# Starting the prompt's attention inside the even layer's last projection unit

## The chip, the core and the metric

The kernel runs on one core of a Trainium2 chip. The metric is device time in microseconds (us) for one execution. TensorE is PE in the profile (PEld is its weight load), VectorE is DVE, ScalarE is ACT, GpSimd is POOL; SP is the engine whose queue issues nearly all DMAs.

## The reference, cut to what matters

One inference step of two layers, on a prompt of 2048 tokens and on 8 sequences of 4 new tokens ("the sample"). The even layer projects its input to a linear-attention branch (A) and to q, k, v, a gate and a forget value of four heads of "forgetting attention" (B, called fox in the code). The odd layer is another linear attention. The part that matters here is the prompt's forgetting attention:

```python
proj = h @ w_in                                  # even layer, all branches
log_fb = log_sigmoid(fb + b_fox)
c = cumsum(log_f, axis=1)                        # per head, over the 2048 tokens
logits = einsum('bthd,bshd->bhts', qi, k) * scale + ci[..., None] - c[:, :, None, :]
logits = where(t >= key_pos, logits, -inf)
p = softmax(logits)
out = einsum('bhts,bshd->bthd', p, v)
```

The sample's attention does the same for its 32 tokens against 128 cached pages of k and of v, read from memory by a page table.

## The kernel before, in words

**Stages.** `phase_even` (L949) computes the even layer's projections in two halves of the tokens, `phase_fox` (L1118) both attentions, `phase_odd` (L1768) the even layer's output projection and the odd layer. A float32 product is made of three float16 products (`mm3`, L468 to L472: high by high, high by low, low by high), so most matmuls of the profile stand at L470, L471 and L472.

**The even layer's units.** Each half runs 16 units of weight columns, in the list `order` of `phase_even`; the last four of it are Bk0, Bv0, Bk1 and Bv1: the keys and values of heads 0 and 1, then those of heads 2 and 3. `staged` (L1044) yields after each piece of a unit and fetches, measures and splits the weights of later units between the pieces. `dense(a, b)` is units a to b - 1 of the half. Of the second half's Bv1, the last unit of all, there are four pieces of 48 matmuls of 128x256 (`proj_tm`); each piece is copied out of PSUM by DVE (L893), and DVE takes its largest value (L902, `vmax`); SP stores it to the output and to `vd` (L907, L910).

**Sums of log f.** When the forget values are there (from Bv0), `log_sigmoid` (L1098) runs; after unit Bk1, `bias_rows` (L1083) makes the cumulative sums with two small matmuls (`cum` L1089, `cumo`), scales them on DVE and stores 64 rows to `cbd` (L1096). The attention reads them back, broadcast, into `cb` (L1165).

**The prompt's attention.** `fox_prompt` (L1153) goes over 16 groups: four heads by four groups G of 512 queries. For group (h, G) it loads q, k, v (`raw`), the bias `cb` and the gate (L1139, L1165, L1174), splits each into two float16 tiles (ACT L1148 and L1149, POOL L1150), and runs four blocks of 128 queries. A block of `scores` (L1185) is G + 1 tiles `s` of up to 512 keys on PE; DVE adds the bias, writes `L` and keeps the maximum (L1203, one pass a tile, two for the tile on the diagonal, where POOL made `cm` from bias and mask, L1189); ACT takes the exponential (L1211); POOL divides by the sum (L1219). `values` (L1222) of the group before runs between these blocks: PE transposes `L` into `pt` (L1239), ACT and DVE split that into `th` and `tl` (L1246, L1247), PE multiplies by v into `fo`. There are two PSUM buffers for `s` and two for `pt`. Group (0, 0) has only four short tiles, group (0, 1) two tiles a block, and so on.

**The sample's attention.** `fox_sample` (L1306) loads pages of k (L1333), transposes each set of four pages on PE (`pkt`, L1363), copies it to SBUF on ACT and DVE (`kts`, L1366 and L1367) and multiplies (`sc`, L1421); later it does the weighted sum over pages of v (`pv`, L1502), with few operations beside PE. Before its first product, DVE scales its q and k (`qs`, `kn`, L1351) and spreads q (`qz`, L1355). Its page buffers (`fs`) lie where the even layer's activations and weights lay.

**What sets the order.** `until(a, ta, b, tb)` (L92) and `mux` draw steps from two generators so that their yielded costs stay in the ratio ta to tb; `until` stops when b ends. This gives each instruction a place in the program; the framework's scheduler then orders every engine's queue by that place and by when it expects inputs to be there. Each engine runs its queue in order. Before, `drain(until(self.prompt, FOX_P, self.fox_sample(fs, pps), FOX_S))` pairs prompt and sample; what is left of the prompt then goes beside `prepare` (in `phase_odd`), which readies the first weights and inputs of the output projection.

**Memory.** Tile pools are stacks on a left and a right side of SBUF, and PSUM has eight banks. Before, all pools of the even layer close together after Bv1, and the attention's pools open then. The attention's `s` tiles take PSUM banks that the projections' `pj` tiles had, so the first `s` waits for the last copies of Bv1.

Of the kernel before, what the change touches and what calls it, by code (L numbers as in the profile page):

```python
# [8 lines left out]
F32 = mybir.dt.float32  # L9
# [6 lines left out]
ALU = mybir.AluOpType  # L16
PSUM = bass.MemoryType.PSUM
DRAM = bass.MemoryType.DRAM

P = 128  # L20
# [19 lines left out]
EWR = 3  # L40
# [8 lines left out]
PG = 25  # L49
# [3 lines left out]
NG = 2  # L53
WSPLIT = 4
FOX_S = 411000.0
FOX_P = 270000.0
LIN3_A = 40000.0
LIN_E = (20000.0, 15000.0)
LIN_O = (31000.0, 23000.0)
# [5 lines left out]
FAR = -3e38  # L65
# [9 lines left out]
def mux(a, ta, b, tb):  # L75

    pa = pb = 0.0
    la = lb = True
    while la or lb:
        if la and (not lb or pa * tb <= pb * ta):  # L80
            c = next(a, None)
            la = c is not None
            pa += c or 0
        else:
            c = next(b, None)
            lb = c is not None
            pb += c or 0
        if c:
            yield c


def until(a, ta, b, tb):  # L92

    pa = pb = 0.0
    while True:
        first = pa * tb <= pb * ta
        c = next(a if first else b, None)
        if c is None and not first:
            return
        if first:  # L100
            pa += c or 0
            if c is None:
                yield from b
                return
        else:
            pb += c
        yield c


def drain(g):  # L110
    for _ in g:
        pass
# [9 lines left out]
class Kern:  # L122
# [825 lines left out]

    def phase_even(self):  # L949
        tc, nc, i = self.tc, self.nc, self.i  # L950
        def pool(name, **kw):
            return tc.tile_pool(name=name, bufs=1, reuse_waits="tile", **kw)

        with pool("act", side="right") as ap, pool("w", side="right") as w0, pool("wl", side="right") as wp1, \
                pool("wk") as wp0, pool("nrm") as n0, pool("stt") as sp, pool("ps", space=PSUM) as pp0:
            wpool = Pool(w0, {"w": 3, "wr": EWR, "rm": 2, "pow": 2, "lr": 8})
            wp = Pool(wp0, {"c4": 7, "sam": 1, "v4": 3, "sg": 3, "pd": 1, "kt": 2, "y": EY, "xpad": 1, "vs": 3,
                            "ss": 2, "rs_t": 2, "rs_r": 2}, Pool(wp1, {"c2": EC2, "th": ETH}))
            pps = Pool(pp0, {"pj": 3, "gr": 2, "st": 1, "o": 2})
            nrm = Pool(n0, {"th": 1, "nss": 4, "rs_t": 4, "rs_r": 4})  # L960
            self.scales2, self.ready, self.fsc, self.logit, self.v_undo = {}, {}, {}, {}, {}
            self.sx_even = self.gain_scale(self.g_even, pps, "pj", "e")
            S1 = sp.tile([P, P], F32, name="Sx")
            S = [(sp.tile([P, P], F32, name=f"S{h}"), S1) for h in range(NH)]
            act = self.alloc_act(ap)
            self.few = wp
            last = iter(())
            order = ["v0", "g0", "qf0", "qf1", "Bq0", "Bg0", "v1", "g1", "qf2", "qf3", "Bq1", "Bg1",
                     "Bk0", "Bv0", "Bk1", "Bv1"]
            us, lins = [], []  # L970

            def beside(x):
                x -= 33
                for n in (1, 2):
                    if 0 <= x - 1 < len(self.later):
                        self.later[x - 1][n]()
                if 0 <= x < len(self.later):
                    self.later[x][0]()

            self.later = []  # L980
            for hf in range(2):
                U, lin = self.even_half(hf, act, wpool, wp, pps, nrm, S)
                us += [U[x] for x in order]
                lins.append(lin)
            for hf in range(2):
                def get_x(c0, m, hf=hf):
                    t = wp.tile([P, HALF + TS], F32, tag="c4", name=f"nx{hf}_{c0}")[:, :D]
                    src = i["x_prompt"][0, hf * HALF + c0 : hf * HALF + c0 + m] if c0 < HALF else \
                        i["x_sample"].rearrange("b t d -> (b t) d")
                    self.last_x = nc.sync.dma_start(t[:m], src)  # L990
                    return t

                def dense(a, b, hf=hf):
                    return self.staged(us, 16 * hf + a, 16 * hf + b, beside)

                lin = lins[hf]
                groups = self.norm_groups(nrm, pps, act, hf, get_x, self.g_even)
                first = self.handover(groups, dense(0, 1), last)
                if hf == 0:
                    groups[0][0]()  # L1000
# [24 lines left out]
                drain(dense(14, 15))  # L1025
                if hf == 1:
                    self.bias_rows(pps, *masks)
                last = dense(15, 16)
            drain(last)

    def later_units(self):
        i = self.i
# [85 lines left out]
    def phase_fox(self):  # L1118
        tc, nc = self.tc, self.nc
        self.fox = ExitStack()  # L1120
        f1, f0 = (self.fox.enter_context(tc.tile_pool(name=x, bufs=2, reuse_waits="tile")) for x in ("fe", "fx"))
        pp1, pp0 = (self.fox.enter_context(tc.tile_pool(name=x, bufs=2, space=PSUM, reuse_waits="tile"))
                    for x in ("fpa", "fpb"))
        if True:
            fx = Pool(f0, {"vh": 5, "vl": 5, "P": 17, "th": 4, "tl": 4, "sg": 3, "y": 1},
                      Pool(f1, {"raw": 6, "caus": 1, "qh": 2, "ql": 2, "kh": 5, "kl": 5, "cb": 2, "st1": 12, "cm": 2}))
            pps = Pool(pp0, {"t": 2, "o": 1, "kt": 2}, Pool(pp1, {"s": 2, "sc": 1}))
            caus = fx.tile([P, P], F32, tag="caus", name="caus")
            nc.gpsimd.memset(caus, 0.0)
            nc.gpsimd.affine_select(caus, caus, [[-1, P]], ALU.is_ge, FAR, base=0, channel_multiplier=1)  # L1130
            with tc.tile_pool(name="fs", bufs=1, side="right", reuse_waits="tile") as s0:
                fs = Pool(s0, {"pg": PG, "kt": 8})
                self.prompt = self.fox_prompt(fx, pps, caus)
                drain(until(self.prompt, FOX_P, self.fox_sample(fs, pps), FOX_S))

    def load(self, fx, src, nm):

# [807 lines left out]
@with_exitstack  # L1945
def hybrid_step_kernel(ctx: ExitStack, tc: tile.TileContext, ins, outs):
    kern = Kern(ctx, tc, ins, outs)
    kern.consts()
    kern.phase_even()
    kern.phase_fox()  # L1950
    kern.phase_odd()


# [17 lines left out]
```

## Time and profile before

| what | us |
|---|---|
| three runs of the kernel | 2399.18, 2390.87, 2393.80; median 2393.8 |
| the profiled execution, its own time | 2395.09 |
| its span, first to last instruction | 2393.4 |
| even layer, 0 to 878.3 | 878.3, PE busy 849.0 |
| attention, 878.3 to 1301 | 422.7, PE busy 393.6 |
| output projection and odd layer, from 1301 | 1092.4, PE busy 1052.0 |

The profiled execution's own time stands 1.7 us above its span, and 1.3 us above the median of the runs. The span is read from the profile's stretches: busy time of each engine in a stretch, and the clock that was granted to PE, where 1.00 is full speed. A matmul's end is modelled, so start-to-start distances are used for what one costs. In the timelines a number in brackets is the idle time of the engine just before the row, and what ended it.

### The profile page before, as it was taken

The numbers are of one execution on the slowest core, as the hardware profiler recorded it, in microseconds if no ns is written. First come the engines' busy times: TensorE is split into PE (matmuls) and PEld (weight loads), VectorE is DVE, ScalarE is ACT, GpSimd is POOL, SyncE is SP. The second block draws the span as 40 slices with busy tenths as digits, with TensorE's granted clock in tenths as the row PEclk, the third lists the DMA queues.
The fourth block names the chain that finished last, engine by engine and source line by source line (L and its number), as shares of the span: only waits on it lengthen the run. The fifth ranks groups of instructions, "written<-read, shape, count | busy, mean of one in ns | idle before, by whom it ended". The sixth has DMA issues, their size and how long they took to land. (4 is left out here: it accounts for less than half of the span.)

```text
span 2393.4 us, 58665 instructions
## 1 busy us (share of the span) xinstructions
PE 2294.6 (96%) x23324; PEld 1635.2 (68%) x23324; DVE 1414.6 (59%) x3345; ACT 1108.6 (46%) x2460; POOL 756.9 (32%) x845
## 2 busy tenths in 40 slices
PE   7999999999999999999999999999999999999998
PEld 5667678854655876655446876777778766666887
DVE  7556556546664548567766463654675644557554
ACT  6434243343433126566676454535543635545333
POOL 2233323112212225234456211432452222322223
PEclk9999999999999999999999999999999999999999
DMA  6231235435431276776864632122156312115453
GB/s 182 79 87 58 85 119 161 147 108 148 147 116 59 82 217 214 254 250 200 264 223 155 191 109 63 50 82 85 44 156 193 107 42 69 43 59 159 154 190 150
DMA packets 297012, 317.24 MB, mean 133 GB/s; under 512 B 39729, under 2 KB 241010, under 8 KB 296738
## 3 DMA queue, kind: packets, MB, share of 16 engines
q1 hardware_dynamic: 295234, 308.98, 41.0%
q8 instruction: 183, 3.00, 0.5%
q0 software_dynamic: 1504, 4.52, 0.5%
q14 instruction: 91, 0.75, 0.1%
HBM read 242.31 MB, written 71.11 MB: 131 GB/s over the span
## 5 line engine op out<-in xcount | busy, mean ns | idle before, releaser
L472 PE MATMUL pt_o<-w_o,act 128*128 128x256 f16 x1024 | 280.4, 274 | 3.6 <-DVE act L1603 3.5
L470 PE MATMUL pt_o<-w_o,act 128*128 128x256 f16 x1024 | 280.7, 274 | 0.9 <-ACT sg1C L526 0.9
L471 PE MATMUL pt_o<-w_o,act 128*128 128x256 f16 x1024 | 280.4, 274 | 0.8 <-POOL w_o L353 0.8
L472 PEld LDWEIGHTS <-act 128*128 128x128 f16 x2304 | 226.3, 98 | 35.4 <-DVE act L1603 4.8
L470 PEld LDWEIGHTS <-act 128*128 128x128 f16 x2304 | 226.3, 98 | 35.2 <-ACT act L465 3.2
L471 PEld LDWEIGHTS <-act 128*128 128x128 f16 x2304 | 226.4, 98 | 31.6 <-issue 2.2
L470 PE MATMUL pt_Cv<-w_Cv,act 128*128 128x256 f16 (+1 forms) x512 | 140.4, 275 | 1.8 <-ACT act L465 1.0
L471 PE MATMUL pt_Cv<-w_Cv,act 128*128 128x256 f16 (+1 forms) x512 | 140.3, 275 | 0.0
L636 POOL TENSOR_TENSOR kA<-kA,fA 128x512 f32<-128x512 f32 (+1 forms) x56 | 79.5, 1421 | 191.5 <-PE gl_A L602 141.5
L472 PE MATMUL pt_Cv<-w_Cv,act 128*128 128x256 f16 (+1 forms) x512 | 140.0, 275 | 0.0
L1211 ACT ACTIVATE L<-L,nm,kc 128x512 f32<-128x512 f32 (+3 forms) x160 | 118.2, 741 | 37.8 <-DVE nm L1209 33.5
L636 POOL TENSOR_TENSOR kC<-kC,fC 128x512 f32<-128x512 f32 (+1 forms) x56 | 81.8, 1461 | 151.7 <-PE gl_C L602 107.2
L1219 POOL TENSOR_SCALAR L<-L,nm 128x512 f32<-128x512 f32 (+3 forms) x160 | 98.8, 631 | 63.3 <-DVE nm L1215 22.5
L1246 ACT ACTIVATE th<-pt 128x512 f16<-128x512 f32 (+3 forms) x159 | 80.7, 527 | 64.8 <-PE pt L1239 64.0
L1247 DVE TENSOR_TENSOR tl<-pt,th 128x512 f16<-128x512 f32 (+3 forms) x159 | 94.6, 608 | 23.3 <-ACT th L1246 22.3
L1239 PE MATMUL pt<-ident,L 128*128 128x128 f32 x544 | 92.7, 283 | 5.8 <-POOL L L1219 2.7
L1239 PEld LDWEIGHTS pt<-ident,L 128*128 128x128 f32 x544 | 68.0, 145 | 32.3 <-DVE tl L1247 8.7
L1363 PEld LDWEIGHTS pkt<-ident,pgcache_fox_k 128*128 128x128 f32 x512 | 58.4, 143 | 43.4 <-issue 25.9
L1363 PE MATMUL pkt<-ident,pgcache_fox_k 128*128 128x128 f32 x512 | 76.0, 281 | 7.3 <-DVE kts L1367 5.2
L470 PE MATMUL pt_Av<-w_Ai,act 128*128 128x256 f16 x256 | 70.2, 275 | 1.3 <-ACT act L465 1.3
L471 PE MATMUL pt_Av<-w_Ai,act 128*128 128x256 f16 x256 | 70.3, 275 | 0.8 <-POOL w_Ai L353 0.8
L472 PE MATMUL pt_Bk<-w_Bk,act 128*128 128x256 f16 x256 | 70.6, 276 | 0.0
(952 smaller groups left out, 6744.4 us busy)
## 6 DMA issues: line engine op xcount, KB each, us to landing
pgcache_fox_k<-in_cache_fox_k SPq DMA_DIRECT2D x128, 256.0 KB, 4.3
pgcache_fox_v<-in_cache_fox_v SPq DMA_DIRECT2D x128, 256.0 KB, 4.0
yr<-yT SPq DMA_DIRECT2D x16, 1024.0 KB, 6.6
nx<-in_x_prompt SPq DMA_DIRECT2D x16, 512.0 KB, 4.7
wr_Aqf<-in_w_in_even SPq DMA_DIRECT2D x64, 128.0 KB, 3.4
wr_o<-in_w_out_even SPq DMA_DIRECT2D x32, 256.0 KB, 4.2
wr_Cv<-in_w_in_odd SPq DMA_DIRECT2D x32, 256.0 KB, 4.1
wr_Cqk<-in_w_in_odd SPq DMA_DIRECT2D x64, 128.0 KB, 2.9
```

The source lines that it names most:

```text
L470: nc.tensor.matmul(ps, lh[0], rh[0], start=first, stop=False)
L471: nc.tensor.matmul(ps, lh[0], rh[1], start=False, stop=False)
L472: return nc.tensor.matmul(ps, lh[1], rh[0], start=False, stop=last)
L636: nc.gpsimd.tensor_tensor(kv[:, :, 0], kv[:, :, 0], t1.to_broadcast([P, nb, w]), ALU.mult)
L1211: self.last_exp = nc.scalar.activation(lt[:, :w], lt[:, :w], AF.Exp, bias=nm[:, 0:1], scale=ib, accum_out=nm[:, 2 + j : 3 + j])
L1219: nc.gpsimd.tensor_scalar(lt[:, :w], lt[:, :w], nm[:, 1:2], 2.0**14, ALU.mult, ALU.mult)
L1239: nc.tensor.transpose(pt[:, w : w + P], rows[b][s // 4][0][:, (s % 4) * P : (s % 4 + 1) * P], self.ident)
L1246: nc.scalar.activation(th[:, a:w], pt[:, a:w], AF.Copy),
L1247: nc.vector.tensor_tensor(tl[:, a:w], pt[:, a:w], th[:, a:w], ALU.subtract)))
L1363: nc.tensor.transpose(pk[:, j * P : (j + 1) * P], pgs[j][:, h * P : (h + 1) * P], self.ident)
```

## The change

The even layer's pools are split in two stacks. On the right stay the activations, the weights and, new there, the PSUM pool `pj` of the projections; on the left lie the rest, and the raw weights (`wr`, before on the right). When only Bv1 is left, the left stack closes and `open_fox` opens the attention's pools in its place, with five PSUM banks (`t`, `o`, `s`); the three others (`kt`, `sc`, for the sample) open once `pj` is closed. Bv1 then runs as the second generator of `until`, with 16000 of the prompt's cost units beside it, at Bv1's 20800. The later pairing of prompt and sample uses 257000 in place of 270000. `bias_rows` now runs after two pieces of unit Bk1, in place of after the unit.

```diff
-FOX_P = 270000.0
+FOX_P = 257000.0
+PRE_P = 16000.0
...
-        with pool("act", side="right") as ap, pool("w", side="right") as w0, pool("wl", side="right") as wp1, \
-                pool("wk") as wp0, pool("nrm") as n0, pool("stt") as sp, pool("ps", space=PSUM) as pp0:
-            wpool = Pool(w0, {"w": 3, "wr": EWR, "rm": 2, "pow": 2, "lr": 8})
+        with ExitStack() as right, ExitStack() as left:
+            ap, w0, wp1 = (pool(right, x, side="right") for x in ("act", "w", "wl"))
+            pj0 = pool(right, "pj", space=PSUM, side="right")
+            wr0 = pool(left, "wr", side="right")
+            wp0, n0, sp = (pool(left, x) for x in ("wk", "nrm", "stt"))
+            pp0 = pool(left, "ps", space=PSUM)
+            wpool = Pool(w0, {"w": 3, "rm": 2, "pow": 2, "lr": 8}, Pool(wr0, {"wr": EWR}))
...
-            pps = Pool(pp0, {"pj": 3, "gr": 2, "st": 1, "o": 2})
+            pps = Pool(pp0, {"gr": 2, "st": 1, "o": 2}, Pool(pj0, {"pj": 3}))
...
-                drain(dense(14, 15))
+                keys = dense(14, 15)
                 if hf == 1:
+                    next(keys)
+                    next(keys)
                     self.bias_rows(pps, *masks)
+                drain(keys)
                 last = dense(15, 16)
-            drain(last)
+            left.close()
+            fx = self.open_fox()
+            drain(until(self.prompt, PRE_P, last, cost))
+        self.phase_fox(*fx)
...
+        more = Pool(None, {"kt": 2, "sc": 1})
+        pps = Pool(pp, {"t": 2, "o": 1, "s": 2}, more)
...
+    def phase_fox(self, pps, more):
+        tc = self.tc
+        more.pool = self.fox.enter_context(tc.tile_pool(name="fpb", bufs=2, space=PSUM, reuse_waits="tile"))
```

The build shows what this does to the queues. Up to the piece of Bk1 at which `cum` now stands, and from the first third of the output projection's first half on, every engine's queue is the same in both; the changed stretch is what the trace has from about 848 us to about 1330 us.

**First place: PE, around the first score tile.** `pt_Bv` is a piece of Bv1, `s000` the first block's tile of head 0, `s010` that of the second block, and `act` the activations as weights of the matmul. Before, the last rows of Bv1 stand ahead of the first score:

```order
L470 MATMUL pt_Bv116_10897<-w_Bv11_10246,act_113 128x256
L471 LDWEIGHTS act_113
L471 MATMUL pt_Bv116_10897<-w_Bv11_10246,act_113 128x256
L472 LDWEIGHTS act_113
L472 MATMUL pt_Bv116_10897<-w_Bv11_10246,act_113 128x256
L470 LDWEIGHTS h_q00_10988
L470 MATMUL s000_11004<-h_k00_10992,h_q00_10988 128x128
L471 LDWEIGHTS h_q00_10988
L471 MATMUL s000_11004<-l_k00_10993,h_q00_10988 128x128
```

Now `s000` stands after six matmuls of the second of Bv1's four pieces (`pt_Bv112`), and 26 more of that piece follow `s010`:

```order
L473 LDWEIGHTS act_119
L473 MATMUL pt_Bv112_10987<-w_Bv11_10252,act_119 128x256
L471 LDWEIGHTS h_q00_10770
L471 MATMUL s000_10786<-h_k00_10774,h_q00_10770 128x128
L472 LDWEIGHTS h_q00_10770
L472 MATMUL s000_10786<-l_k00_10775,h_q00_10770 128x128
L473 LDWEIGHTS l_q00_10771
L473 MATMUL s000_10786<-h_k00_10774,l_q00_10771 128x128
L471 LDWEIGHTS h_q00_10770
L471 MATMUL s010_10863<-h_k00_10774,h_q00_10770 128x256
```

All score tiles of groups (0, 0) and (0, 1), the values of (0, 0) and the first four transposes of (0, 1) have moved in among Bv1's matmuls. Behind Bv1's last matmul come the scores of group (0, 2) with the values of (0, 1), and the sample's first `pkt` only after the first blocks of (0, 3).

**Second place: DVE, where Bv1 ends.** `Bv116` is the copy of Bv1's last piece, `L000`, `L080` and the like the passes over score tiles (ISA rows of one column are the read-out of the maximum). Before, the copy and its maximum end Bv1, and the attention begins behind them:

```order
L893 TENSOR_SCALAR Bv116_10946<-pt_Bv116_10897,kc_67 128x512
L902 TENSOR_REDUCE vmax_68<-Bv116_10946 128x1
L261 TENSOR_REDUCE kc_67<-vmax_68 128x1
L1203 ISA L000_11008,mx00_11003<-s000_11004,cm00_11001 128x128
L1203 ISA mx00_11003 128x1
L1209 TENSOR_SCALAR nm00_11010<-mx00_11003,kc_67 128x1
```

Now they stand between the passes of the blocks 7 and 8 of head 0:

```order
L1223 ISA L071_11113,mx07_11102<-s071_11109,cb0_10764,mx07_11102 128x384
L1223 ISA mx07_11102 128x1
L894 TENSOR_SCALAR Bv116_11330<-pt_Bv116_11281,kc_67 128x512
L1223 ISA L071_11113,mx07_11102<-s071_11109,cm07_11100,mx07_11102 128x128
L1223 ISA mx07_11102 128x1
L903 TENSOR_REDUCE vmax_68<-Bv116_11330 128x1
L1229 TENSOR_SCALAR nm07_11170<-mx07_11102,kc_67 128x1
L1223 ISA L080_11197,mx08_11192<-s080_11193,cb0_10764 128x512
```

The second pass over `s071` and the pass over `s080`, which free the two `s` buffers, are now queued behind the copy.

**Third place: DVE, where the sample begins.** `qs`, `kn` and `qz` are the sample's q and k, `kts` a copy of transposed pages. Before, they stand behind block 7 of head 0:

```order
L1351 TENSOR_SCALAR qs_11226<-qs_11226,kc_67 128x64 x2
L1214 TENSOR_REDUCE nm06_11191<-nm06_11191 128x1
L1351 TENSOR_SCALAR kn_11227<-kn_11227,kc_67 128x64 x2
L1367 COPY kts001_11318<-pkt001_11313 128x512
L1209 TENSOR_SCALAR nm07_11297<-mx07_11212,kc_67 128x1
L1262 SCALAR_TENSOR_TENSOR fy000_11320<-fo00_11082,kc_67,fsg00_10986 128x512
L1355 TENSOR_TENSOR qz_11238<-qs_11226,bmask_823 128x256 x3
```

Now they stand five blocks later, behind the third full tile of block 12:

```order
L1371 TENSOR_SCALAR qs_11518<-qs_11518,kc_67 128x64 x2
L1371 TENSOR_SCALAR kn_11519<-kn_11519,kc_67 128x64 x2
L1267 TENSOR_TENSOR tl0106_11435<-pt0106_11431,th0106_11434 128x256
L1387 COPY kts001_11652<-pkt001_11647 128x512
L1267 TENSOR_TENSOR tl0107_11444<-pt0107_11441,th0107_11443 128x128
L1375 TENSOR_TENSOR qz_11530<-qs_11518,bmask_829 128x256 x4
L1223 ISA L0123_11593,mx012_11499<-s0123_11589,cm012_11497,mx012_11499 128x128
```

The four scalings still stand ahead of the first copies `kts`, now all in one run, and ahead of the last pass over block 12.

More of the change, by code (lines that the diff above doesn't have):

```diff
@@ L950, in phase_even, with pool @@
         tc, nc, i = self.tc, self.nc, self.i
-        def pool(name, **kw):
-            return tc.tile_pool(name=name, bufs=1, reuse_waits="tile", **kw)
-        with pool("act", side="right") as ap, pool("w", side="right") as w0, pool("wl", side="right") as wp1, \
-                pool("wk") as wp0, pool("nrm") as n0, pool("stt") as sp, pool("ps", space=PSUM) as pp0:
-            wpool = Pool(w0, {"w": 3, "wr": EWR, "rm": 2, "pow": 2, "lr": 8})
+        def pool(stack, name, **kw):
+            return stack.enter_context(tc.tile_pool(name=name, bufs=1, reuse_waits="tile", **kw))
+        with ExitStack() as right, ExitStack() as left:
[5 more added lines that the diff above has]
+            wpool = Pool(w0, {"w": 3, "rm": 2, "pow": 2, "lr": 8}, Pool(wr0, {"wr": EWR}))
             wp = Pool(wp0, {"c4": 7, "sam": 1, "v4": 3, "sg": 3, "pd": 1, "kt": 2, "y": EY, "xpad": 1, "vs": 3,
                             "ss": 2, "rs_t": 2, "rs_r": 2}, Pool(wp1, {"c2": EC2, "th": ETH}))
-            pps = Pool(pp0, {"pj": 3, "gr": 2, "st": 1, "o": 2})
+            pps = Pool(pp0, {"gr": 2, "st": 1, "o": 2}, Pool(pj0, {"pj": 3}))
             nrm = Pool(n0, {"th": 1, "nss": 4, "rs_t": 4, "rs_r": 4})
@@ L1116, in log_sigmoid, with open_fox @@
         nc.vector.scalar_tensor_tensor(zz, q, -2.0, zz, ALU.mult, ALU.add)
-    def phase_fox(self):
+    def open_fox(self):
         tc, nc = self.tc, self.nc
         self.fox = ExitStack()
[L1121 to L1134, printed above, removed]
@@ new lines, in pool @@
+        def pool(name, **kw):
+            return self.fox.enter_context(tc.tile_pool(name=name, bufs=2, reuse_waits="tile", **kw))
+        f1, f0, pp = pool("fe"), pool("fx"), pool("fpa", space=PSUM)
+        fx = Pool(f0, {"vh": 5, "vl": 5, "P": 17, "th": 4, "tl": 4, "sg": 3, "y": 1},
+                  Pool(f1, {"raw": 6, "caus": 1, "qh": 2, "ql": 2, "kh": 5, "kl": 5, "cb": 2, "st1": 12, "cm": 2}))
+        more = Pool(None, {"kt": 2, "sc": 1})
+        pps = Pool(pp, {"t": 2, "o": 1, "s": 2}, more)
@@ new lines, in open_fox @@
+        caus = fx.tile([P, P], F32, tag="caus", name="caus")
+        nc.gpsimd.memset(caus, 0.0)
+        nc.gpsimd.affine_select(caus, caus, [[-1, P]], ALU.is_ge, FAR, base=0, channel_multiplier=1)
+        self.prompt = self.fox_prompt(fx, pps, caus)
+        return pps, more
+    def phase_fox(self, pps, more):
+        tc = self.tc
+        more.pool = self.fox.enter_context(tc.tile_pool(name="fpb", bufs=2, space=PSUM, reuse_waits="tile"))
+        with tc.tile_pool(name="fs", bufs=1, side="right", reuse_waits="tile") as s0:
+            fs = Pool(s0, {"pg": PG, "kt": 8})
+            drain(until(self.prompt, FOX_P, self.fox_sample(fs, pps), FOX_S))
@@ L1949, in hybrid_step_kernel @@
     kern.phase_even()
-    kern.phase_fox()
     kern.phase_odd()
```

## The prediction

> **What bounds the kernel now.** I read the page's busy times first, then the stretches around the end of the even layer, then PE's timeline and waits there, then DVE's groups of equal shape, and last the transfers that feed the moved work.
>
> ```profile
> PE 2294.6 (96%) x23324; PEld 1635.2 (68%) x23324; DVE 1414.6 (59%) x3345; ACT 1108.6 (46%) x2460; POOL 756.9 (32%) x845
> ```
>
> PE is busy for 2294.6 of the span's 2393.4 us. The change takes no matmul away, so it can gain only where PE idles or is granted less than its full clock. In the stretches the columns are: length, busy time of PE, PEld, DVE, ACT and POOL (instructions in brackets), the granted clock of PE, the share of the DMA engines, GB/s.
>
> ```profile
> 857.00:878.30 21.30, 21.30 (x194) 18.58 (x191) 5.26 (x10) 3.23 (x5) 3.13 (x4) 1.00 0.68 225
> 878.30:908.00 29.70, 22.59 (x112) 12.36 (x111) 21.91 (x82) 16.38 (x39) 19.30 (x29) 0.77 0.96 320
> 1100.00:1300.00 200.00, 184.35 (x1188) 96.78 (x1181) 141.67 (x476) 135.54 (x316) 115.81 (x169) 0.97 0.63 202
> 880.60:884.00 3.40, 1.89 (x8) 0.65 (x8) 2.96 (x19) 2.44 (x7) 3.31 (x7) 0.99 1.06 332
> 884.00:890.80 6.80, 6.12 (x21) 2.92 (x22) 3.14 (x14) 4.95 (x12) 5.79 (x8) 0.50 0.87 274
> 897.60:901.00 3.40, 1.38 (x10) 1.02 (x10) 3.40 (x8) 1.22 (x3) 1.66 (x3) 1.00 1.03 358
> 901.00:907.80 6.80, 5.58 (x26) 3.31 (x26) 3.99 (x15) 2.70 (x6) 4.32 (x7) 0.50 0.87 276
> 1200.00:1203.40 3.40, 2.81 (x18) 1.42 (x15) 3.15 (x12) 1.38 (x4) 3.38 (x5) 1.00 0.77 264
> ```
>
> The first row is Bv1: PE is full, the other engines are nearly empty. The second is the start of the attention, where this turns round: PE idles 29.70 - 22.59 = 7.1 us, and in two stretches of 6.8 us its clock is 0.50. There PE was busy 6.12 + 5.58 = 11.7 us, of which half, 5.9 us, is the price of the clock. So **before loses 13.0 us between 878.3 and 908**, and that is nearly all that this change can reach. Each drop follows a window of 3.4 us in which PE was busy 56% (1.89) and 41% (1.38); after one at 83% (2.81) the clock stayed at 1.00.
>
> The idle part, in PE's timeline (start, duration, engine, line, tiles; in brackets idle time and its releaser) and its waits (total, times, longest) from 876 to 920:
>
> ```profile
> 878.19 0.27 PE L472 MATMUL pt_Bv<-w_Bv,act 128*128 128x256 f16 x1
> 879.46 0.22 PE L470 MATMUL s<-h_k,h_q 128*128 128x128 f16 x1 [0.99 <-DVE Bv L893]
> ...
> 894.82 1.04 PE L1363 MATMUL pkt<-ident,pgcache_fox_k 128*128 128x128 f32 x8
> ...
> 896.87 0.38 PE L470 MATMUL s<-h_k,h_q 128*128 128x512 f16 x1
> 897.08 0.38 PE L471 MATMUL s<-l_k,h_q 128*128 128x512 f16 x1
> 899.62 1.10 PE L1363 MATMUL pkt<-ident,pgcache_fox_k 128*128 128x128 f32 x8 [2.16 <-DVE kts L1367]
> ```
>
> ```profile
> PE pkt L1363 <- DVE kts L1367: 3.4, 2, 2.2
> PE s L470 <- DVE Bv L893: 1.0, 1, 1.0
> PE s L470 <- DVE mx L1203: 0.7, 2, 0.4
> ```
>
> Two causes stand here: the ramp (one block of short tiles after another, each waiting for a pass of DVE), and the sample's first copies `kts`, which cost 3.4 us in two waits.
>
> **The change part by part.** *The sums of log f* go ahead by 97 matmuls of Bk1, which at 21.30 / 194 = 0.11 us for such a matmul (Bv1's stretch) is 10.7 us. Nothing is added; the two small matmuls are the same. What hangs on them:
>
> ```profile
> 860.07 0.28 DVE L1090 COPY cmask<-cum 64x128 f32<-64x128 f32 x1 [2.99 <-PE cum L1089]
> ```
>
> ```profile
> 864.24 0.52 SPq L1096 DMA_DIRECT2D cbd<-cmask  x1
> ...
> 866.61 0.32 SPq L1165 DMA_DIRECT2D cb<-cbd  x1
> ...
> 884.79 3.05 SPq L1333 DMA_DIRECT2D pgcache_fox_k<-in_cache_fox_k  x6
> ```
>
> ```profile
> 871.90 0.87 POOL L1189 TENSOR_TENSOR cm<-cb,caus 128x128 f32<-128x128 f32 x2 [0.46 <-DMA cb<-cbd]
> ```
>
> Moved by 10.7 us, the store `cbd` is issued at about 853.5, the load `cb` at 855.9, and the first `cm` starts at 861.2. `s000` stands 54 matmuls behind Bv1's first (which starts at about 857.3), so at 857.3 + 54 x 0.11 = 863.3. The bias is there 2 us early; PE's term in Bv1 is 0. Were it late, `s000` and `s010` would fill both `s` buffers and everything behind them in PE's queue would wait, Bv1's matmuls too: up to 1.5 us. SP's loads for the groups (0, 0) and (0, 1) now stand ahead of Bv1's stores, and the pages of the sample behind its last. In the trace of before the pages go out 6.5 us after Bv1's last matmul (884.79 after 878.3), and the first `pkt` starts 10.0 us later without an idle time; at the same distance they are there 16.5 us behind Bv1, and the stretch below gives `pkt` a place 18 to 19 us behind it. On ACT the last copy of Bk1 now stands behind a split that waits for a load; only keys of heads 2 and 3 wait for that copy, and ACT is busy for 3.23 us of Bv1's 21.30: 0.
>
> *The work beside Bv1.* In PE's queue there are the scores of (0, 0) and (0, 1), the values of (0, 0) and 14 transposes. From the 0.21 us between the two `s` matmuls of 128x512 above, shorter ones by their width, these are 5.8 us of scores, 1.6 of values, and at 1.04 / 8 = 0.13 a transpose 1.8: 9.2 us. Bv1 so ends at about 878.2 + 9.2 = 887.5 to 888.5; this work is not added, it is missing behind Bv1. DVE had 5.26 us of work in 21.3; it gets 9 us more, in a stretch of 30. Loss: **0, at most 1.5**.
>
> *The stretch behind Bv1*, up to the first `pkt`, has prompt work alone: 12 full score tiles and three shorter ones (3 x 0.215 a full tile, 8.7 us), 22 transposes (2.4 to 2.9) and 18 matmuls of values (3.7): 14.8 us for PE. DVE, by its groups from 878.3 to 1300 (busy, mean ns):
>
> ```profile
> L1247 DVE TENSOR_TENSOR tl<-pt,th 128x512 f16<-128x512 f32 x106 | 71.6, 685 | 22.1 <-ACT th L1246 21.3
> L1367 DVE COPY kts<-pkt 128x512 f32<-128x512 f32 x64 | 44.0, 687 | 37.6 <-PE pkt L1363 37.2
> L1203 DVE CUSTOM_DVE_ANT_0 L<-s,cb,mx 128x512 f32<-128x512 f32 x48 | 35.9, 747 | 8.3 <-PE s L472 7.1 <-DVE mx L1203 0.2
> L1203 DVE CUSTOM_DVE_ANT_0 L<-s,cb 128x512 f32<-128x512 f32 x48 | 32.8, 684 | 10.2 <-PE s L472 9.4 <-POOL cm L1189 0.4
> L1203 DVE CUSTOM_DVE_ANT_0 L<-s,cm,mx 128x128 f32<-128x128 f32 x60 | 20.9, 348 | 4.6 <-PE s L472 0.4 <-DVE tl L1247 0.2 <-PE pt L1239 0.2
> L1203 DVE DVE_READ_ACCUMULATOR2_ANT mx<- 128x1 f32 x208 | 17.2, 83 | 0.0
> ```
>
> The queue of after has in this stretch 5 first passes (5 x 0.684), 6 second ones (6 x 0.747), 5 on the diagonal (5 x 0.348), 1.4 us of partial passes, 19 read-outs (1.6), 6 `tl` (4.0), Bv1's last copy and its maximum (0.75 + 0.69 from the same stretch of the trace) and 2.7 us of small ones: 20.7 us. DVE's rows overlap by about 0.08 us each, which takes off up to 3.5. So **DVE is the bound there**: it needs 17.2 to 20.7 us where PE needs 14.8, and PE loses **2.4 to 6 us; I take 4**. The copy out of `pt_Bv` hides nothing now: behind it on DVE wait the passes that free both `s` buffers.
>
> *The sample's start.* Before, PE waited 3.4 us for `kts`, because DVE scaled `kn` and `qs` ahead of it:
>
> ```profile
> 896.07 0.67 DVE L1351 TENSOR_SCALAR qs<-qs,kc 128x64 f32<-128x64 f32 x2
> ...
> 896.73 2.23 DVE L1351 TENSOR_SCALAR kn<-kn,kc 128x64 f32<-128x64 f32 x2
> ```
>
> ```profile
> 896.65 1.16 POOL L1150 TENSOR_TENSOR l_q<-raw_q,h_q 128x512 f16<-128x512 f32 x1
> ```
>
> These four operations are only moved, in one run ahead of the first `kts`. At the price of `qs` they would be 1.3 us, at that of both rows 2.9, and one pass can lie ahead of the copy. **1.0 to 3.3; I take 2.5**, nearest to the row of `kn`. [...]
>
> *The clock.* With 14.8 of some 19 us, PE is busy about 78% of the stretch behind Bv1, nearer to the window that kept its clock (83%) than to those that lost it (56%, 41%); around `kts` one such window may still come. One drop cost 6.12 / 2 = 3.1 to 3.4 us: **0 to 3.4; I take 1.5**. [...]
>
> *The later pairing.* With less of the prompt left and FOX_P at 257000, prompt and sample end about where they ended. From 1100 to 1300 PE idles 15.65 us, in many small waits; a shift of the pairing can add or spare one of up to 4 us. I take a gain of 1.
>
> **The sum.** Before lost 13.0. After loses 0 + 4 + 2.5 + 1.5 = 8.0. The gain is 5.0, with the later 1 it is 6. The profiled execution took 2395.1, its span 2393.4; 2395.1 - 6 = 2389.1, and the median of the runs stands 1.3 lower, so **2388**.
>
> **The rivals.** *Nearly all is hidden* (R2): DVE's rows overlap fully, and `kts` waits 1.0. The loss is 2.4 + 1.0 = 3.4, the gain 9.6, with 0 to 4 from the pairing 10 to 14: 2380 to 2384. For it speaks that Bv1's stretch has DVE at a quarter; against it that DVE, ACT and POOL are all near full behind it.
>
> *The ramp only moves* (R1): all terms at their upper ends, 1.5 + 6 + 3.3 + 3.4 = 14.2, against 13.0 before; with the pairing -2 to +2, 2392 to 2397. For it speaks that DVE's load behind Bv1 is 1.4 times PE's; against it that the shortest blocks, those with the least PE work per pass, are gone from there.
>
> *The sample is the path* (R3, slower). Its page buffers lie where Bv1's activations and weights lie, so its loads cannot start before Bv1's end, which comes 9 to 10 us later. If the sample's length, from its pages at 884.79 to its last product, is set by its own transfers and not by PE, its end and all behind it move by 10: 2393.8 + 10 = 2404.
>
> ```profile
> L1502 PE MATMUL pv<-pgcache_fox_v,pT x256: 592/592/1061, 1111.1 to 1261.4; 128*16 128x512 f32 x128
> ...
>   DMA pgcache_fox_v<-in_cache_fox_v: 1.1, 2
> ```
>
> Against it: PE waits for its pages only 1.1 us in two waits, and the DMA share from 1100 to 1300 is 0.63, so PE's queue sets its pace, and less prompt work now stands in that queue. It decides from the point where page waits are over 10 us. That the change would not do what it says is excluded: the rows of the queues show the scores inside Bv1.
>
> **How the numbers follow.** The forecast, a gain of 2 to 10, is 2384 to 2392, with a chance of 0.58; R1 0.16, R2 0.14, R3 0.12. The range takes in the forecast, R2 with 1 us of the pairing below it, and R1 with a stall of 4 us above it, 2379 to 2401, and leaves out R3. A measurement of this kernel tells about 0.3%, 7.2 us, from no change. Faster than 2386.6 are all of R2 and, of the forecast's gains of 2 to 10, those over 7.2, a third of it at most: 0.14 + 0.22 = 0.36. Slower than 2401 is R3, 0.12. The rest, 0.52, is within.
>
> **What would show it.** Right: score tiles from about 863 inside Bv1, no idle time of PE up to its end at about 888; behind it short waits of `s` for `mx` that add up to some 4 us with DVE over 90% busy; a `pkt` that waits about 2.5 us for `kts`; at most one drop of the clock. Wrong: waits for `cb` or `cm` inside Bv1; a clock at 0.50 for more than 7 us behind it (R1); first pages later than 897, waits of `pkt` or `pv` for pages (R3); a new wait of over 4 us between 1100 and 1300, at the end of the pairing.

## The result, and the profile after

The change made the kernel slower: 2406.05 us median (2398.61 to 2412.42, 12 runs) against 2394.8 (2390.59 to 2399.99, 12 runs), a ratio of 1.0043 with a 95% interval of 1.0031 to 1.0055. The forecast was 2388, its range 2379 to 2401. The rival on the slow side (R3, the sample as the path) had been priced at 2404 and given 0.12.

The profiled execution took 2412.42, 6.4 above its median. Part of that is older than the change. Up to the middle of Bk1 both kernels have the same queues, and the last `lf` of DVE (the forget values of Bv0) already comes 3.4 us later. In the two timelines, before and then after (lines of the changed kernel are 1 to 20 higher):

```profile
833.62 0.22 DVE L888 SCALAR_TENSOR_TENSOR lf<-pt_Bv,kc,bfox 128x4 f32<-128x4 f32 x1
```

```profile
837.04 0.22 DVE L889 SCALAR_TENSOR_TENSOR lf<-pt_Bv,kc,bfox 128x4 f32<-128x4 f32 x1
```

So times below are counted from this `lf` wherever two kernels are compared. The same stages in windows (length, busy time of PE, PEld, DVE, ACT, POOL, granted clock, DMA share, GB/s), before: Bv1, then up to the first `pkt`, the sample's stretch to its last `pv` over cached pages, the rest of the attention, and the first 36.9 us of the output projection.

```profile
857.00:878.30 21.30, 21.30 (x194) 18.58 (x191) 5.26 (x10) 3.23 (x5) 3.13 (x4) 1.00 0.68 225
878.30:894.80 16.50, 12.89 (x59) 6.38 (x58) 11.89 (x54) 9.90 (x25) 10.97 (x18) 0.79 0.98 322
894.80:1261.40 366.60, 346.56 (x2437) 198.85 (x2437) 249.90 (x778) 232.81 (x526) 167.74 (x266) 0.98 0.71 232
1261.40:1307.90 46.50, 41.06 (x297) 29.54 (x290) 37.86 (x106) 32.77 (x72) 33.72 (x40) 0.96 0.41 134
1307.90:1344.80 36.90, 36.14 (x349) 31.89 (x346) 16.78 (x31) 23.96 (x44) 15.76 (x14) 1.00 1.05 331
```

And after:

```profile
860.40:890.90 30.50, 30.50 (x260) 25.09 (x259) 16.63 (x62) 14.47 (x34) 15.66 (x24) 1.00 0.73 254
890.90:909.20 18.30, 16.34 (x86) 8.15 (x84) 16.59 (x60) 15.66 (x39) 15.11 (x25) 1.00 0.92 295
909.20:1277.00 367.80, 342.23 (x2408) 197.35 (x2410) 244.90 (x747) 222.07 (x498) 158.55 (x249) 0.98 0.69 224
1277.00:1313.10 36.10, 31.00 (x233) 21.69 (x226) 27.23 (x72) 24.50 (x54) 23.02 (x26) 1.00 0.36 116
1313.10:1350.00 36.90, 29.23 (x259) 23.79 (x257) 17.15 (x29) 23.74 (x45) 17.66 (x16) 0.91 0.99 328
```

Read row against row. In Bv1 PE stays full with 9.0 us of the prompt's products added. In the second row the clock is 1.00 where it was 0.79. The third row is the surprise: it has 6.0 us less of the prompt's products (185.4 against 191.4, their start-to-start times at full clock added up), yet it is 1.2 us longer. In the last row the output projection, full before, has PE idle for 7.7 us and a clock of 0.91.

**The start.** The waits of PE from 891 to 925, the first rows:

```profile
PE s L471 <- DVE mx L1223: 1.9, 5, 0.5
PE fo L471 <- ACT th L1266: 1.3, 1, 1.3
```

The waits for `kts` and for Bv1's copy are gone from here. What scales the sample's q and k, on DVE, with POOL's row beside it:

```profile
910.17 0.98 DVE L1371 TENSOR_SCALAR qs<-qs,kc 128x64 f32<-128x64 f32 x2
910.71 0.63 DVE L1371 TENSOR_SCALAR kn<-kn,kc 128x64 f32<-128x64 f32 x2
```

```profile
909.42 1.15 POOL L1170 TENSOR_TENSOR l_k<-raw_k,h_k 128x512 f16<-128x512 f32 x1
```

Before, POOL's `l_q` (from 896.65) and, right behind it, this row lay beside the two operations of `kn`:

```profile
897.76 1.16 POOL L1150 TENSOR_TENSOR l_k<-raw_k,h_k 128x512 f16<-128x512 f32 x1
```

Now `qs` lies beside `l_k` and takes 0.98 where it took 0.67, and `kn`, which begins when `l_k` has ended (910.57), takes 0.63 in place of 2.23. So in both traces the longer of the two is the one that lies beside a split of POOL; what links them is not shown. (POOL's memset `sel`, 0.52 us from 910.55, lies beside `kn` at these 0.63.)

**The end.** PE's waits from 1313 to 1430, the first rows, after:

```profile
PE pt_o L471 <- ACT w_o L353: 3.9, 1, 3.9
PE pS_o L515 <- DVE sam_o L510: 1.5, 1, 1.5
PE pt_o L473 <- POOL act L1620: 1.0, 2, 0.8
```

Before, the largest from 1308 to 1420 were these:

```profile
PE nt L434 <- DVE act L466: 1.9, 3, 0.9
PE pt_Cv L470 <- ACT act L465: 1.0, 1, 1.0
```

PE waits for a split weight `w_o`, but ACT only reaches that split after the last piece of the input, which waits for its load `yr`:

```profile
1336.05 0.35 ACT L1622 ACTIVATE act<-yr,kc 128x64 f16<-128x64 f32 x1 [5.13 <-DMA yr<-yT]
...
1337.31 0.71 ACT L352 ACTIVATE wr_o<-wr_o,kc 128x512 f32<-128x512 f32 x1
```

SP issued that load, the fifth `yr`, behind six loads of `row`:

```profile
1320.07 0.37 SPq L1609 DMA_DIRECT2D yr<-yT  x1
1320.54 3.89 SPq L1853 DMA_DIRECT2D row<-in_x_prompt  x6
1326.64 0.38 SPq L1609 DMA_DIRECT2D yr<-yT  x1
```

Before, the first of the two loads in this row is the fourth `yr`, and the second, the fifth, went out at 1315.3, ahead of the `row` loads:

```profile
1309.95 5.76 SPq L1589 DMA_DIRECT2D yr<-yT  x2
```

The last values `ys` of the sample, before and then after:

```profile
1275.57 0.40 DVE L1516 TENSOR_TENSOR ys<-oT,sgs 128x16 f32<-128x16 f32 x4
```

```profile
1286.50 0.33 DVE L1536 TENSOR_TENSOR ys<-oT,sgs 128x16 f32<-128x16 f32 x3
```

The `yr` loads come one after another through two buffers, and all but the first come behind the sample's end. The fifth fetches the sample's own piece, of which `ys` is a part and whose scale needs `ys`. Counted from the end of `ys`, the second `yr` went out after 20.5 us before and 20.8 now, the fifth after 39.4 and 39.8. So the load is as late as `ys` is; the six loads ahead of it are not what delays it. The last piece was split (by ACT, into its first float16 tile) 15.1 us after the attention's last product before, and 24.1 us after it now.

The profile's 14.3 us (17.7 at the last matmul, less the 3.4 that were there already) divide so: the time up to the first `pkt` is 11.0 longer with 15.3 more of the prompt's products, a gain of 4.3; the sample's stretch loses 7.3 (by the third rows PE idles 25.6 us in it where it idled 20.0, at a mean clock of 0.98 in both); the rest of the attention gains 1.1; the output projection's first part, up to the copy out of its first transposed row piece `prT`, loses 9.8 (112.9 against 103.1); behind it lie another 2.7.

### The profile page after: what moved, and what is told of

Same layout as the page of the kernel before. It is cut to its first block, busy times and chain, and to the rows that moved or that the text cites. A ratio compares the mean times of both kernels' runs of the same rounds, so it can differ in the third digit from the quotient of the medians.

```text
span 2410.7 us, 58664 instructions
## 1 busy us (share of the span) xinstructions
PE 2298.5 (95%) x23324; PEld 1636.6 (68%) x23324; DVE 1420.0 (59%) x3345; ACT 1110.0 (46%) x2460; POOL 757.7 (31%) x845
## 5 line engine op out<-in xcount | busy, mean ns | idle before, releaser
L637 POOL TENSOR_TENSOR kA<-kA,fA 128x512 f32<-128x512 f32 (+1 forms) x56 | 79.5, 1420 | 193.2 <-PE gl_A L603 142.9
L1231 ACT ACTIVATE L<-L,nm,kc 128x512 f32<-128x512 f32 (+3 forms) x160 | 118.3, 741 | 37.2 <-DVE nm L1229 37.0
L1259 PEld LDWEIGHTS pt<-ident,L 128*128 128x128 f32 x544 | 66.9, 144 | 38.9 <-DVE tl L1267 15.3
```

The source lines that it names most:

```text
L637: nc.gpsimd.tensor_tensor(kv[:, :, 0], kv[:, :, 0], t1.to_broadcast([P, nb, w]), ALU.mult)
L1231: self.last_exp = nc.scalar.activation(lt[:, :w], lt[:, :w], AF.Exp, bias=nm[:, 0:1], scale=ib, accum_out=nm[:, 2 + j : 3 + j])
L1259: nc.tensor.transpose(pt[:, w : w + P], rows[b][s // 4][0][:, (s % 4) * P : (s % 4 + 1) * P], self.ident)
```

## The experiments

Three theories stood first. **A**: the sample ends late, and the output projection's inputs, which follow its end, are late. **B**: the moved tiles or the split pools cost the time. **C**: the new FOX_P costs it.

The first table has, from each kernel's profile, the times that are not the prompt's products (those are 235.6 us in every one): "start" up to the first `pkt`, "sample" to the last `pv` over pages, "rest" to the attention's last product, "output" from there to DVE's copy out of the first `prT`. "Last input" is how long after the attention's last product the last input piece of the output projection was split; "cover" is the time from the last `ys` to that product. The ratio and its interval are the estimate from all runs of the kernel and of the kernel before, which ran beside it on the chip; it differs from the quotient of the two medians by up to 0.0009.

| kernel | ratio (95% interval) | start | sample | rest | cover | last input | output |
|---|---|---|---|---|---|---|---|
| before | 1 | 52.6 | 175.2 | 10.7 | 32.0 | 15.1 | 103.1 |
| changed | 1.0043 (1.0031 to 1.0055) | 48.3 | 182.4 | 9.7 | 26.4 | 24.1 | 112.9 |
| e1 | 1.0031 (1.0013 to 1.0049) | 48.2 | 178.0 | 13.6 | 44.8 | 9.9 | 102.5 |
| e2 | 1.0072 (1.0053 to 1.0091) | 56.9 | 174.9 | 7.2 | 13.1 | 35.2 | 122.3 |
| e3 | 1.0027 (1.0014 to 1.0040) | 52.2 | 182.5 | 12.6 | 46.3 | 10.4 | 102.7 |
| e4 | 1.0036 (1.0023 to 1.0048) | 52.7 | 180.7 | 14.4 | 48.1 | 10.6 | 102.0 |
| e5 | 1.0010 (1.0000 to 1.0020) | 48.3 | 174.9 | 14.4 | 43.4 | 10.5 | 102.4 |
| e6 | 1.0050 (1.0030 to 1.0069) | 55.4 | 173.5 | 20.2 | 50.1 | 10.4 | 102.5 |
| e7 | 1.0027 (1.0016 to 1.0037) | 52.6 | 170.2 | 12.3 | 21.5 | 26.3 | 113.8 |
| e8 | 0.9993 (0.9981 to 1.0006) | 48.3 | 181.0 | 11.1 | 37.2 | 13.2 | 102.6 |
| e9 | 1.0044 (1.0032 to 1.0057) | 51.2 | 172.8 | 16.5 | 36.6 | 19.5 | 109.2 |
| e10 | 1.0027 (1.0016 to 1.0038) | 54.2 | 175.6 | 9.0 | 29.6 | 14.9 | 104.0 |
| e11 | 0.9969 (0.9957 to 0.9981) | 48.3 | 169.6 | 13.9 | 35.8 | 11.8 | 102.1 |
| e12 | 0.9999 (0.9986 to 1.0013) | 52.6 | 172.1 | 14.3 | 42.1 | 10.0 | 102.4 |

A single profile can stand 6 us from its kernel's median (that of the changed kernel stands 6.4 above, that of e1 6.1 below), so the columns tell where time is, and the ratios tell how much.

### The pace, the pools and the moved work apart

e1 is the changed kernel with less of the prompt beside the sample:

```diff
-FOX_P = 257000.0
+FOX_P = 240000.0
```

> The changed kernel with FOX_P at 240000 in place of 257000: less of the prompt beside the sample, more behind it. Theory A (the sample begins 10 us later, is not shorter, and the output projection's weights and inputs, which are fetched when it ends, are late): the sample ends about 8 us earlier than in the changed kernel and more prompt work lies behind it to cover the fetches, so the stall at the start of the output projection (12.4 us of PE idle time in its first 137 us, 4.3 before) falls to about half: 2396 to 2400. Theory B (the moved score tiles and the split pools cost the time themselves): as the changed kernel, 2404 to 2408. Theory C (the lower FOX_P is what costs): worse still, 2412 to 2420.

Measured 2402.37 (2394.6 to 2411.19) beside 2396.13. The stall at the output projection is gone (102.5), the sample's stretch has only part of its loss back. Between A and B; C is out as written.

e2 goes the other way:

```diff
-FOX_P = 257000.0
+FOX_P = 270000.0
```

> The changed kernel with the old FOX_P of 270000. Theory A: the sample ends some 6 us later still and next to no prompt work is left behind it, so the output projection starts with a longer stall: 2410 to 2416. Theory B: as the changed kernel, 2404 to 2408. Theory C: the loss is gone, 2386 to 2394.

Measured 2412.41 (2408.14 to 2417.74), as A said. The cover is 13.1 us, and the output projection's part takes 122.3.

e3 keeps the pools, the early sums and FOX_P, and takes the prompt from beside Bv1, all but its first step:

```diff
-PRE_P = 16000.0
+PRE_P = 1.0
```

> The changed kernel with PRE_P at 1: pools split and opened ahead of Bv1, sums of log f early, FOX_P 257000, but of the prompt only its first step beside Bv1. Bv1 ends as before. Theory A: the sample starts and ends on time with more prompt work behind it than in the kernel before: 2388 to 2396. Theory B, if the split pools cost: 2400 to 2406; if the moved tiles cost: 2390 to 2396. Theory C: 2404 to 2412.

e4 is the kernel before with the new pace alone:

```diff
-FOX_P = 270000.0
+FOX_P = 257000.0
```

> The kernel before with FOX_P at 257000 and nothing else. Theory A: the sample ends some 6 us earlier with more prompt work behind it, 2388 to 2396. Theory B: the same, 2390 to 2396. Theory C: 2402 to 2410.

e3 took 2402.24, e4 2402.89, both beside 2396.13. A was wrong on both. They agree with each other, so the pools and the early sums cost nothing that shows, which takes that half out of B. And the pace of 257000 alone costs 6.8 us, as C had it: both lose 5 to 7 us in the sample's stretch and 2 to 4 in the rest, and nothing at the output projection. By its ratio e4 loses nearly as much as the changed kernel (1.0036 and 1.0043), but in other places: the changed kernel has 9.8 us of its loss at the output projection. And with the moved work a higher FOX_P is worse, not better (e2): it takes the loss out of the sample's stretch (174.9) and adds more to the start and the output projection. So C alone does not explain the changed kernel. From e3 to the changed kernel, with FOX_P equal, the attention's last product comes 6.8 us earlier by the profiles (482.8 to 476.0) and the output part takes 10.2 us longer: the moved work does save time, and gives back more.

### The cover by itself

e5 is the changed kernel with only the cost of one step over the pages of v changed. Everything up to these pages is ordered as in the changed kernel; beside them stands less of the prompt, which is then left for behind the sample:

```diff
-PV_C = 5860.0
+PV_C = 5300.0
```

> The changed kernel with PV_C at 5300 in place of 5860, so that up to the pages of v everything is ordered as in the changed kernel and beside these pages stands a tenth less of the prompt. Theory A, as the first four runs sharpened it (the output projection is ready some 33 us after the sample's last value, however much prompt work is left to cover that; the changed kernel has 26.4 us of it): the sample's end comes about 9 us earlier, the prompt's end stays, the stall at the start of the output projection goes: 2395 to 2399. Theory B (that stall belongs to the way in which the moved work or the split pools order the queues): 2403 to 2408, as the changed kernel. Theory C (what costs is a pace that differs from 270000 in the sample's stretch): 2404 to 2410.

Measured 2397.66 (2393.04 to 2403.18) beside 2394.56, as A said: about 8 of the 11 us are gone. By the profiles the output part is 10.5 us shorter than in the changed kernel; the sample's stretch is 7.5 shorter as well, and the rest 4.7 longer. PE's waits in the output projection's first part are now these:

```profile
PE nt L435 <- DVE act L467: 1.3, 2, 0.9
PE pt_Cv L471 <- DVE few_o L520: 0.7, 1, 0.7
```

No wait for `w_o` or a piece of the input stands there.

e6 tries the same with the old FOX_P:

```diff
-FOX_P = 257000.0
+FOX_P = 270000.0
-PV_C = 5860.0
+PV_C = 4800.0
```

> The changed kernel with the old FOX_P of 270000 and PV_C at 4800. With FOX_P 270000 alone the sample's stretch lost nothing against the kernel before, but only 13.1 us of prompt were left behind the sample. PV_C at 4800 takes about 19 us of the prompt from beside the pages of v. Theory A: the cover is 32 us again, no stall at the output projection, and the gain of 4 us at the start of the attention is left over: 2389 to 2396. Theory B: 2408 to 2414, as with FOX_P 270000 alone. Theory C: 2395 to 2402.

Measured 2404.73 (2399.19 to 2413.07): a miss for A in the sum. The stall went, from 122.3 to 102.5, but the rest of the attention took 9.5 us more than in the kernel before (20.2), and the start had lost its gain already with FOX_P 270000: more of the prompt stands ahead of the first `pkt` there, without the sample beside it.

e7 puts the stall into the kernel before, by the same constant:

```diff
-PV_C = 5860.0
+PV_C = 6500.0
```

> The kernel before with PV_C at 6500 in place of 5860 and nothing else: 11 to 12 us more of the prompt beside the pages of v, so the sample ends later and 32 us of cover become 20. Theory A: the stall that the changed kernel shows appears in the kernel before too, 9 to 12 us: 2404 to 2409. Theories B and C (which tie the stall to the moved work, or to FOX_P): 2393 to 2399.

Measured 2401.28 (2395.85 to 2404.09) beside 2394.56. The stall is there without any of the change's edits, in the waits from 1303 to 1420:

```profile
PE pt_o L470 <- ACT act L1602: 5.0, 2, 3.8
PE nt L434 <- DVE act L466: 1.2, 2, 0.8
PE pt_o L472 <- POOL act L1600: 0.9, 2, 0.6
```

The output part takes 113.8, 10.7 more than before. The time is 2.7 us below A's range and 2.3 above that of B and C; the waits decide for A. In the profile, with more of the prompt beside the pages of v, the sample's own time is 5.0 us shorter, which A had not counted.

e8 is a pace between:

```diff
-FOX_P = 257000.0
+FOX_P = 249000.0
```

> The changed kernel with FOX_P at 249000, between the two that were measured. Theory A: a little more cover than at 257000, 32 to 33 us, so next to no stall at the output projection; the sample's stretch loses 3 to 7 us by its own waits: 2397 to 2403. Theory B: 2404 to 2408. Theory C, with a loss that grows with the distance from 270000: 2405 to 2412.

Measured 2395.31 (2387.72 to 2398.98): level with the kernel before, 1.7 below A's range, with the cover at 37.2 and no stall.

### Can the start's gain be seen?

A stands against **D**: whatever delays Bv1 delays the sample and comes back. e9 moves more of the prompt:

```diff
-FOX_P = 257000.0
+FOX_P = 240000.0
-PRE_P = 16000.0
+PRE_P = 24000.0
```

> The changed kernel with half as much again of the prompt beside Bv1 (PRE_P 24000) and FOX_P at 240000, so that about as much is left behind the sample as with FOX_P 249000. Theory A (the start gains, and it shows as long as 32 us or more are left behind the sample): more of the start's short blocks lie beside Bv1, where prompt work costs only its own PE time, the stall at the output projection stays away: 2390 to 2395. Theory D (each us by which the prompt's work delays Bv1 delays the sample and comes back behind it, so that the start's gain is never seen): 2397 to 2402.

Measured 2406.64 (2401.9 to 2411.58). Neither range held it, D's was nearer, and the run did not do what it was made for: beside Bv1 stand 9.0 us of the prompt's products, as with 16000, and the rest of the additional part went behind Bv1, ahead of the first `pkt`, which came 14 us later than in e8. The last input comes 19.5 us after the attention, and part of the stall is back, although the cover is 36.6 us: the 32 of theory A do not decide by themselves, the time of the last input does.

e10 moves less of it:

```diff
-FOX_P = 257000.0
+FOX_P = 259000.0
-PRE_P = 16000.0
+PRE_P = 8000.0
```

> The changed kernel with half as much of the prompt beside Bv1 (PRE_P 8000) and FOX_P at 259000, again with about the same left behind the sample. Theory A: half of the start's gain, no stall: 2393 to 2398. Theory D: better than with 16000 or 24000, 2390 to 2394.

Measured 2400.88 (2391.21 to 2406.8), a miss for both. 6.8 us of products lie beside Bv1, the start gains nothing (54.2). Its profile shows no reason for a loss of that size; it is one of the faster executions of a kernel that spreads over 16 us.

e11 takes both settings by half:

```diff
-FOX_P = 257000.0
+FOX_P = 253000.0
-PV_C = 5860.0
+PV_C = 5600.0
```

> The changed kernel with FOX_P at 253000 and PV_C at 5600, between the two settings that took the stall away (249000 alone, PV_C 5300 alone). Theory A: more than 32 us left behind the sample, no stall: 2392 to 2398, next to the kernel before. Theory D: 2396 to 2402.

Measured 2387.62 (2382.86 to 2389.82, 6 runs) beside 2393.84: a ratio of 0.9969, interval 0.9957 to 0.9981, faster than both kernels and below A's range. The start keeps its 4.3 us, there is no stall, and the sample's own time is the shortest of all. PE's waits from 1302 to 1405:

```profile
PE nt L435 <- DVE act L467: 1.0, 2, 0.6
PE pt_Cv L471 <- DVE few_o L520: 0.6, 1, 0.6
```

e12 asks whether that is the pacing alone (theory **E**), on the kernel before:

```diff
-PV_C = 5860.0
+PV_C = 5600.0
```

> The kernel before with PV_C at 5600, the setting of the fastest kernel so far, and nothing else: some 5 us of the prompt go from beside the pages of v to behind the sample. Theory A (the fastest kernel's gain is that of the moved start, seen because the stall is gone): the kernel before has no such stall to lose, and prompt work behind the sample runs slower than beside it, so 2394 to 2400. Theory E (its gain is that of the pacing alone, and the kernel before has it as well): 2386 to 2390.

Measured 2396.33 beside 2396.7, a ratio of 0.9999 (0.9986 to 1.0013). This setting by itself brings the kernel before nothing, as A said; E is out for PV_C alone. For the pair of constants it stays untested: FOX_P at 253000 was not run without the moved work, with or without PV_C at 5600. What speaks against E there is that 257000 cost 6.8 us in the kernel before (e4).

## Why the prediction was wrong

**The sums of log f: right.** `s000` was forecast for 863.3; in the profile it starts 866.65, which less 3.4 is 863.25. PE has no idle time in Bv1, and e3 against e4 shows no price of the early sums.

**The work beside Bv1: right.** 9.0 us of products against 9.2 forecast, Bv1's last matmul starts at 890.63, or 887.2 once the 3.4 are taken off, and there is no loss of PE there.

**The stretch behind Bv1: right.** Forecast were 4 us over the products' 14.8, and 3.7 over 14.9 came. DVE was busy for 16.59 of 18.30 us, 91%. The sign given for it came in part: the waits of `s` for `mx` up to 925 add up to 1.9 us and not to 4; PE idles 18.30 - 16.34 = 2.0 of the 3.7.

**The sample's start and the clock: too high.** 2.5 and 1.5 were taken; no wait for `kts` shows up to 925, and the clock stayed at 1.00 (890.9 to 928.0). The term of `kts` rested on `kn` at its price beside `l_q`, 2.23 us, and `kn` now ran with no such row beside it, in 0.63. Over 878.3 to 908 before and its counterpart, 13.0 us of loss became 4.5 (idle time from 877 to 927; in the clock there is none), a gain of 8.5 where 5.0 was forecast; 4.3 of it lie ahead of the first `pkt`, the others in the first part of the sample's stretch.

**The later pairing: the step that failed.** The prediction let "prompt and sample end about where they ended" and took a gain of 1, with a stall of up to 4 us either way. That held for the prompt (its last product 1.9 us later), not for the sample: `ys` came 7.4 us later, since Bv1 ended 9.0 later by the `lf` mark and the stretch of the sample was no shorter in spite of 6.0 us less of the prompt. Outside of R3 the prediction asked when the attention ends, and never what starts from the sample's end. The output projection's last input is one of those things. It takes a chain of loads and splits from `ys` on, and had been hidden by 32.0 us of cover, at 15.1 us past the attention's last product. Up to 15.1 the table shows an output part of 102 to 104, at 19.5 it is 109.2, at 24.1 to 26.3 it is 113 to 114, at 35.2 it is 122.3. That column separates the kernels with the stall from those without; e5 and e7 take the stall out of the changed kernel and put it into the kernel before by one constant. So the stall is shown, not only argued, and it is 9.8 us by the profile; neither run prices it alone, since both also shorten the sample's stretch (by 7.5 and 5.0).

The other half of this step is the new FOX_P, counted in that gain of 1: in the kernel before it cost 6.8 us by itself (e4), most of it in the sample's stretch, where the changed kernel loses 7.3. That the loss goes with this setting is shown; by what mechanism is open. The signs that the prediction gave for being wrong did not come: no wait of PE between 1100 and 1300 is longer than 2.5 us, and the first pages were asked for at 897.56, which less the 3.4 is 894.1. The loss at the output projection lies behind the window in which it said to look.

**The rival R3: right in its place, wrong in its condition, near in its price by luck.** It said that the sample's length would not shrink, that everything behind it would move by 10, and 2404. The length did not shrink. But the prompt's last product moved by 1.9, not by 10, and the profile's loss is made of other terms: 9.8 and 7.3 lost, 4.3 and 1.1 gained, 2.7 open. And it was to decide when the waits for pages pass 10 us, and these are 3.5 us:

```profile
PE pv L1522 <- DMA pgcache_fox_v<-in_cache_fox_v: 3.5, 2, 2.5
```

So by that sign the sample's transfers were not the limit. Its chance was cut to 0.12 by a row about the wrong resource: PE can set the pace of the sample and the sample's end can still be what the next stage waits for. (A third of 0.58, the part of the forecast's chance that counts as visibly faster, is 0.19 and not the 0.22 that stands there.)

**What stays open.** The sample's own time runs from 169.6 to 182.5 us in the table, and all three kernels with FOX_P at 257000 and PV_C at 5860 are at its upper end, with or without the moved work, and e8 with them. e5 has the changed kernel's order up to the pages of v and is 7.5 us shorter in the stretch, though it waits for pages as long. No single wait carries this: the waits are many and small. At that setting PE idles 25 to 26 us in the stretch, against 20.0 before and 19.2 in e11; the clock adds to the scatter, since it falls to 0.50 three times there before, four times in the changed kernel and twice in e11. Which constant gives which sum was not found. The last part of the changed kernel's profile, 2.7 us behind that `prT`, and the 5 us by which the medians of e1 and e10 exceed what their profiles show, are not explained either.

## What to carry to other kernels

Work moved ahead to fill an engine moves everything behind it, and what counts is not when the stage ends but when each thing ends that the next stage starts from: list these, with the time by which each is covered, before costing the move. A change in one place of a paced pair wants the pace set anew: the same edit gave 1.0043 with one pair of constants and 0.9969 with another. And a rival's condition should be put on the event that the next stage waits for, not on the resource that one suspects.

## What the runs showed that was not expected

The clock fell after thin windows again: before, 1.38 and 1.89 us of PE in 3.4 us were followed by 0.50; after, one with 1.02 lies in the stall at the output projection, and the two windows behind it have 0.63 and 0.50.

```profile
1337.00:1340.40 3.40, 1.02 (x24) 0.55 (x25) 2.66 (x7) 3.40 (x9) 0.57 (x2) 1.00 1.07 295
1340.40:1343.80 3.40, 0.58 (x2) 0.25 (x2) 0.57 (x2) 3.40 (x7) 0.90 (x1) 0.63 1.09 347
1343.80:1347.20 3.40, 3.09 (x15) 2.23 (x15) 3.30 (x6) 3.40 (x8) 2.55 (x3) 0.50 0.44 141
```

Behind Bv1 the thinnest such window has 2.12 of 3.4 us (62%), and its clock stayed at 1.00:

```profile
891.40:894.80 3.40, 2.12 (x10) 0.84 (x11) 3.17 (x13) 1.60 (x4) 3.37 (x6) 1.00 0.82 245
```

But thin windows did not always cost it. In the changed kernel one with 1.74 us (51%), thinner than the 1.89 that was followed by a drop before, kept 1.00:

```profile
1296.88:1300.29 3.41, 1.74 (x16) 1.45 (x15) 0.99 (x4) 3.41 (x9) 3.41 (x3) 1.00 0.00 0
1300.29:1303.70 3.41, 2.40 (x17) 1.66 (x17) 3.29 (x6) 3.24 (x7) 3.41 (x3) 1.00 0.00 0
```

The windows are cut by hand, and the two traces show no share of busy time at which the clock falls. In and behind the stall at the output projection the clock was 0.50 from 1341.3 to 1348.1, and PE was busy for 4.58 us of that: by an estimate, half of these 4.58, the lower clock cost about 2.3 us there, beside the 7.7 us of idle time.
